# Masks of local attention scores: written into PSUM by VectorE instead of added by TensorE, and maxima taken for two heads together

## The chip, the cores and the metric

The kernel runs on one core of a Trainium2 chip. The metric is device time in microseconds (us); what is compared is the median of several runs. The engines are named as in the profile: PE is TensorE (its weight loads stand apart as PEld), DVE is VectorE, ACT is ScalarE, POOL is GpSimd, SP issues most DMAs.

## The reference

Two layers, each with three token mixers beside each other; the change touches one of them, attention over a window. There are 256 context tokens and 1024 latent tokens in 8 blocks of 128, with 8 query heads and 2 key heads of 64. A latent query sees all context keys and the latent keys at most 128 positions away, that is its own block, and parts of the block before and the block after:

```
s_win = jnp.einsum('bnigrd,bnjgd->bngrij', qb, kw).astype(jnp.float32) * scale
s_win = jnp.where(valid[None, :, None, None], s_win, NEG)
s_ctx = jnp.einsum('bnigrd,bjgd->bngrij', qb, k_c).astype(jnp.float32) * scale
p_ctx, p_win = sink_softmax(sink_g, [s_ctx, s_win])
```

`sink_softmax` is a softmax with one more logit per head. The third mixer, dense attention ("axial"), has no mask.

## The kernel before

Matrix products take fp32 operands as high and low parts, two or three products each. `attention` works through items: a pair of heads (`t`, 0 to 3) by a chunk of queries (`c`: 0 is the 256 context queries, 1 and 2 are 512 latent queries each), the window items first, then the axial ones. Layer 0 has 12 window items, layer 1, which drops the context queries, has 8; 16 window items in all have masks (`c` 1 and 2, four `t`, two layers).

`main` does an item in groups, a PSUM bank each, two banks (`psS`, 64 and 65 in the rows of the order) in turn. A masked item has 11 groups: four over context keys (512 columns, no mask), four over 384 columns for one head, and three that hold 256 columns for each of both heads. The last seven are masked. `scores` of a group issues two products (L1007, L1008) for each head, then the mask products (L1010: the identity times a bfloat16 mask of 0 and -1e30, added onto the bank), two exponentials on ACT (L1014, and L1015 rounded), and on DVE their difference `att_Pl` (L1016). The products with V (L1026) of a group follow two groups later (`LAG`). A masked 384-column group has two masks of 128 columns; a group of both heads has one mask for each head, of 128 columns, or 256 columns in one of the three groups (the last one when `c` is 1). That is 7 mask products per head, 14 an item.

`maxes` finds, for the item after, the maximum of each query's scores: rows of the same scores the other way round (L905), masked in the same manner (also L905), and a `reduce_max` on DVE (L906), in two banks (`mx`, 62 and 63) in turn, one head at a time.

`interleave` lays the steps of `main` and of the side work (`maxes` of the next item, projections of items to come) beside each other by their costs. After that a scheduler of the framework decides the final order on each engine; each engine then runs its own list in order.

Of the kernel before, what the change touches and what calls it, by code (L numbers as in the profile page):

```python
# [10 lines left out]
BF16 = mybir.dt.bfloat16  # L11
AF = mybir.ActivationFunctionType
ALU = mybir.AluOpType
# [12 lines left out]
NEG = -1e30  # L26
# [92 lines left out]
class Net:  # L119
# [26 lines left out]
    def consts(self):  # L146
# [11 lines left out]
        self.jt = c[:, C_JT:C_JT + 2]  # L158
        cb = one("cb", 512, BF16)
        self.identb = cb[:, 0:128]  # L160
        self.mask = cb[:, 128:512]
        nc.vector.tensor_copy(self.identb, self.ident)
        mk = self.tmp(384)
        self.dma(mk, I["mask"])
        nc.vector.tensor_copy(self.mask, mk)
        self.nh = one("nh", 8)
# [511 lines left out]
    def attention(self, l, ctxq, begin):  # L678
# [204 lines left out]
        def maxes(it, boundary=False):  # L883
# [3 lines left out]

            def one(h, qt, i, k0, kn, b, b0, b1):
                mt = it["mt"].rearrange("p (h q x) -> p h q x", h=2, q=4)
                ps = mx.next()  # L890
                if boundary and i not in kc:
                    x = self.tmp(kn)
                    self.dma(x, self.kd_ax[:, k0:k0 + kn])
                    kc[i] = P.get("Ph", 512, F32R)
                    nc.scalar.copy(kc[i][:, :kn], x)
                a = rows[h] if boundary else slice(0, 128)
                rhs = kc[i][a, :kn] if boundary else Kd[h][:, k0:k0 + kn]
                ops = [(ps[:, :kn], it["X"][a, h, 128 * qt:128 * qt + 128], rhs)]
                if win and i:
                    if b0 < b:  # L900
                        ops.append((ps[:, 0:128], self.identb, self.mask[:, 256:384]))
                    if b1 > b:
                        ops.append((ps[:, kn - 128:kn], self.identb, self.mask[:, 0:128]))
                for x, op in enumerate(ops):
                    nc.tensor.matmul(*op, start=x == 0, stop=x == len(ops) - 1)  # L905
                nc.vector.reduce_max(mt[:, h, qt, i:i + 1], ps[:, :kn], AX.X)  # L906

            it["ns"] = 1 if c == 0 else 2 if win else 3
            for i in range(it["ns"]):
                for qt in range(nq):  # L910
# [7 lines left out]
                    else:  # L918
                        b = 4 * (c - 1) + qt
                        b0, b1 = max(b - 1, 0), min(b + 1, 7)  # L920
                        k0, kn = 256 + 128 * b0, 128 * (b1 - b0 + 1)
                    for h in (0, 1):
                        yield kn / 1000, lambda x=(h, qt, i, k0, kn, b, b0, b1): one(*x)

# [34 lines left out]
        def groups(it):  # L959
# [7 lines left out]
            q0 = 4 * (c - 1)  # L967
            Mh, Ml = self.mask[:, 0:128], self.mask[:, 256:384]
            twos = []
            for b in range(max(q0 - 1, 0), min(q0 + 4, 7) + 1):  # L970
                lo, hi = max(b - 1, q0), min(b + 1, q0 + 3)
                if lo == hi:
                    if b < q0:
                        p = (2 + b, 0, 256, ((self.mask[:, 0:256], 0, 256),))
                    else:
                        p = (2 + b, 256, 256, ((self.mask[:, 128:384], 0, 256),))
# [15 lines left out]
        def main(it, after_scores=None):  # L992
# [5 lines left out]
            def scores(g):  # L998
# [4 lines left out]
                for (h, kt, q0, nq, ms) in g:  # L1003
# [3 lines left out]
                    nc.tensor.matmul(o, Kd[h][:, ksl], it["X"][:, h, q0:q0 + nq], start=True, stop=False)  # L1007
                    nc.tensor.matmul(o, Kl[h][kr, ksl], it["Y"][kr, h, q0:q0 + nq], start=False, stop=not ms)  # L1008
                    for i, (m, mo, mn) in enumerate(ms):
                        nc.tensor.matmul(ps[:, off + mo:off + mo + mn], self.identb, m, start=False,  # L1010
                                         stop=i == len(ms) - 1)
                    off += nq
# [512 lines left out]
```

## Time and profile before

| | |
|---|---|
| median of 3 runs | 3158.52 us (3156.61 to 3161.45) |
| the profiled execution: its time, its span | 3155.12 us, 3153.3 us |
| PE busy, PEld busy | 97%, 80% of the span |
| DVE, ACT, POOL busy | 58%, 37%, 25% |
| TensorE clock granted, mean | 0.993 of full speed |

Busy time of PE counts a product until its result is complete, so that neighbours overlap: the cost of a product is read from one start to the next. A row of the timeline gives start, duration, engine, line, operation, output<-input, shape and count; the brackets at its end say how long the engine sat idle before, and what ended that.

### The profile page before, as it was taken

The numbers are of one execution on the slowest core, as the hardware profiler recorded it, in microseconds if no ns is written. First come the engines' busy times: TensorE is split into PE (matmuls) and PEld (weight loads), VectorE is DVE, ScalarE is ACT, GpSimd is POOL, SyncE is SP. The second block draws the span as 40 slices with busy tenths as digits, with TensorE's granted clock in tenths as the row PEclk, the third lists the DMA queues.
The fourth block names the chain that finished last, engine by engine and source line by source line (L and its number), as shares of the span: only waits on it lengthen the run. The fifth ranks groups of instructions, "written<-read, shape, count | busy, mean of one in ns | idle before, by whom it ended". The sixth has DMA issues, their size and how long they took to land. (4 is left out here: it accounts for less than half of the span.)

```text
span 3153.3 us, 44619 instructions
## 1 busy us (share of the span) xinstructions
PE 3043.7 (97%) x16794; PEld 2514.3 (80%) x16794; DVE 1827.7 (58%) x3404; ACT 1180.6 (37%) x2295; POOL 773.2 (25%) x597
## 2 busy tenths in 40 slices
PE   7999989999999999999999999899999999999998
PEld 4889778887778787888887888777776777888886
DVE  5774737677875876412245674546678776753233
ACT  3311124455555555112223312134545555642231
POOL 2342541223222110111211343442222212002130
PEclk9999999999999999999999999999999999999999
DMA  6121211112111113512153121211112111143223
GB/s 245 41 65 54 71 56 33 46 46 68 44 54 44 41 45 100 157 38 67 41 200 111 53 66 60 66 56 48 44 51 66 47 38 58 44 151 97 66 66 99
DMA packets 135704, 224.10 MB, mean 71 GB/s; under 512 B 19648, under 2 KB 45248, under 8 KB 135488
## 3 DMA queue, kind: packets, MB, share of 16 engines
q1 hardware_dynamic: 126848, 207.10, 20.9%
q10 hardware_dynamic: 8640, 14.16, 1.2%
q8 instruction: 131, 2.15, 0.3%
q14 instruction: 85, 0.70, 0.1%
HBM read 181.52 MB, written 39.60 MB: 70 GB/s over the span
## 5 line engine op out<-in xcount | busy, mean ns | idle before, releaser
L323 PE MATMUL bank<-H_h,S_whi 128*128 128x512 f32 (+1 forms) x2536 | 960.1, 379 | 0.6 <-ACT H_h L415 0.6
L324 PE MATMUL bank<-H_h,S_whi 128*128 128x512 f32 (+1 forms) x2536 | 937.9, 370 | 5.7 <-DVE H_h L420 4.0
L325 PE MATMUL bank<-H_h,S_wlo 128*128 128x512 f32 (+1 forms) x2536 | 935.8, 369 | 0.0
L323 PEld LDWEIGHTS bank<-H_h,S_whi 128*128 128x128 f32 x2536 | 480.8, 190 | 80.2 <-issue 7.7
L325 PEld LDWEIGHTS bank<-H_h,S_wlo 128*128 128x128 f32 x2536 | 479.8, 189 | 77.0 <-issue 0.6
L324 PEld LDWEIGHTS bank<-H_h,S_whi 128*128 128x128 f32 x2536 | 480.9, 190 | 74.4 <-DVE H_h L420 5.1
L1016 DVE TENSOR_TENSOR att_Pl<-att_P,att_Ph 128x512 fp32r<-128x512 f32 (+1 forms) x512 | 376.9, 737 | 257.7 <-ACT att_Ph L1015 233.8
L1014 ACT ACTIVATE att_P<-bank 128x512 f32<-128x512 f32 (+1 forms) x512 | 299.1, 584 | 450.3 <-PE bank L1008 326.4
L906 DVE TENSOR_REDUCE S_s<-bank 128x1 f32<-128x256 f32 (+2 forms) x672 | 350.7, 535 | 115.2 <-PE bank L905 110.5
L303 ACT CAST S_whi<-S_raw 128x512 fp32r<-128x512 f32 x320 | 198.0, 621 | 525.7 <-PE bank L324 457.6
L1026 PE MATMUL bank<-att_Ph,att_V 128*128 128x512 f32 (+2 forms) x1152 | 332.1, 372 | 0.0
L305 POOL TENSOR_TENSOR S_wlo<-S_raw,S_whi 128x512 fp32r<-128x512 f32 x130 | 171.9, 1324 | 619.8 <-ACT S_whi L303 527.1
L1015 ACT ACTIVATE att_Ph<-bank 128x512 fp32r<-128x512 f32 (+1 forms) x512 | 297.1, 580 | 3.8 <-PE bank L905 3.1
L305 DVE TENSOR_TENSOR S_wlo<-S_raw,S_whi 128x512 fp32r<-128x512 f32 x190 | 153.7, 811 | 160.8 <-ACT S_whi L303 159.8
L905 PE MATMUL bank<-att_Kd,att_X 128*128 128x256 f32 (+2 forms) x644 | 217.0, 343 | 22.8 <-DVE S_s L906 12.0
L1026 PEld LDWEIGHTS bank<-att_Ph,att_V 128*128 128x128 f32 x1152 | 201.3, 190 | 29.6 <-issue 0.6
L1007 PE MATMUL bank<-att_X,att_Kd 128*128 128x512 f32 (+2 forms) x576 | 214.7, 373 | 0.0
L1008 PE MATMUL bank<-att_Y,att_Kl 68*128 68x512 f32 (+2 forms) x576 | 210.5, 366 | 0.3 <-DVE att_Y L955 0.3
L1026 PE MATMUL bank<-att_Pl,att_V 128*128 128x512 f32 (+2 forms) x576 | 205.3, 364 | 0.7 <-DVE att_Pl L1016 0.7
L1230 POOL TENSOR_TENSOR mrg_Y<-S_t,mrg_Y 128x512 f32<-128x512 f32 x64 | 95.8, 1496 | 423.3 <-DVE S_t L1229 423.2
L323 PE MATMUL bank<-mrg_G,S_whi 128*128 128x512 f32 (+1 forms) x480 | 176.7, 371 | 5.7 <-ACT mrg_G L1239 5.3
L1229 DVE SCALAR_TENSOR_TENSOR S_t<-S_t,bank 128x512 f32<-128x512 f32 x64 | 44.0, 687 | 235.7 <-PE bank L325 230.8
(207 smaller groups left out, 4380.8 us busy)
## 6 DMA issues: line engine op xcount, KB each, us to landing
S_raw<-in_win SPq DMA_DIRECT2D x216, 256.0 KB
S_t<-rd SPq DMA_DIRECT2D x108, 128.0 KB
gd<-S_t SPq DMA_DIRECT2D x48, 256.0 KB
thd<-att_th ACTq DMA_DIRECT2D x48, 256.0 KB
S_raw<-in_wp SPq DMA_DIRECT2D x48, 256.0 KB
S_t<-thd SPq DMA_DIRECT2D x48, 256.0 KB
init_wm<-in_wmod SPq DMA_DIRECT2D x16, 512.0 KB
retb_wg<-in_wmod SPq DMA_DIRECT2D x32, 256.0 KB
```

The lines of the kernel that those rows point to most:

```text
L305: self.weng.tensor_tensor(lw, raw, h.bitcast(F32), ALU.subtract)
L323: nc.tensor.matmul(ps[0][:, :n], a, xhi[k], start=k == 0, stop=False)
L324: nc.tensor.matmul(ps[0][:, :n], a, xlo[k], start=False, stop=False)
L325: nc.tensor.matmul(ps[0][:, :n], b, xhi[k], start=False, stop=k == kts - 1)
L905: nc.tensor.matmul(*op, start=x == 0, stop=x == len(ops) - 1)
L906: nc.vector.reduce_max(mt[:, h, qt, i:i + 1], ps[:, :kn], AX.X)
L1007: nc.tensor.matmul(o, Kd[h][:, ksl], it["X"][:, h, q0:q0 + nq], start=True, stop=False)
L1008: nc.tensor.matmul(o, Kl[h][kr, ksl], it["Y"][kr, h, q0:q0 + nq], start=False, stop=not ms)
L1014: nc.scalar.activation(p, ps[:, :off], AF.Exp, scale=0.125)
L1015: nc.scalar.activation(ph, ps[:, :off], AF.Exp, scale=0.125)
L1016: nc.vector.tensor_tensor(pl, p, f32(ph), ALU.subtract)
L1026: nc.tensor.matmul(pvb[h][:, q0:q0 + nq], Vf[:, kt, 192 * lo + 64 * h:192 * lo + 64 * h + 128], x, start=not started[h], stop=stop)
```

## The change

In `main` the mask products are gone. VectorE writes -1e30 into the bank itself, `copy_predicated` with a byte mask (`outside`) and one constant broadcast over the columns, after the group's score products and before its exponentials: 14 copies an item, 12 of 128 columns and 2 of 256. In `maxes` the masks stay products, but masked steps take both heads at once: two score products, then the masks of both, then two maxima. Three small instructions on DVE at the start make the byte mask and the constant.

```diff
+        nc.vector.tensor_copy(self.mask[:, 0:128], mk[:, 0:128])
+        nc.vector.tensor_copy(self.mask[:, 128:256], mk[:, 256:384])
+        self.outside = one("outside", 384, mybir.dt.uint8)
+        nc.vector.tensor_scalar(self.outside, mk, 0.0, None, ALU.is_lt)
+        self.neg = one("neg", 8)
+        nc.vector.memset(self.neg, NEG)
...
-            def one(h, qt, i, k0, kn, b, b0, b1):
+            def some(hs, qt, i, k0, kn, b, b0, b1):
...
-                for x, op in enumerate(ops):
-                    nc.tensor.matmul(*op, start=x == 0, stop=x == len(ops) - 1)
-                nc.vector.reduce_max(mt[:, h, qt, i:i + 1], ps[:, :kn], AX.X)
+                pss = [mx.next() for h in hs]
+                for h, ps in zip(hs, pss):
...
+                    nc.tensor.matmul(ps[:, :kn], it["X"][a, h, 128 * qt:128 * qt + 128], rhs, start=True,
+                                     stop=not masks)
+                for ps in pss:
+                    for x, (o, m) in enumerate(masks):
+                        nc.tensor.matmul(ps[:, o:o + 128], self.identb, m, start=False, stop=x == len(masks) - 1)
+                for h, ps in zip(hs, pss):
+                    nc.vector.reduce_max(mt[:, h, qt, i:i + 1], ps[:, :kn], AX.X)
...
-                    for h in (0, 1):
-                        yield kn / 1000, lambda x=(h, qt, i, k0, kn, b, b0, b1): one(*x)
+                    for hs in (((0, 1),) if win and i else ((0,), (1,))):
+                        yield len(hs) * kn / 1000, lambda x=(hs, qt, i, k0, kn, b, b0, b1): some(*x)
...
-                    nc.tensor.matmul(o, Kl[h][kr, ksl], it["Y"][kr, h, q0:q0 + nq], start=False, stop=not ms)
-                    for i, (m, mo, mn) in enumerate(ms):
-                        nc.tensor.matmul(ps[:, off + mo:off + mo + mn], self.identb, m, start=False,
-                                         stop=i == len(ms) - 1)
+                    nc.tensor.matmul(o, Kl[h][kr, ksl], it["Y"][kr, h, q0:q0 + nq], start=False, stop=True)
+                    for m, mo, mn in ms:
+                        nc.vector.copy_predicated(ps[:, off + mo:off + mo + mn], m,
+                                                  self.neg.to_broadcast([128, mn]))
```

Lines of the changed program are 6 to 11 higher: L905 becomes L911 (scores) and L915 (masks) of `maxes`, L906 becomes L917, L1007, L1008 become L1018, L1019, L1016 becomes L1027, L1026 becomes L1037; the copies are L1021.

Three places of the order show what moved. The first is PE in `maxes` of the first masked window item (bank 62 is one head, bank 63 the other). Before, a step of each head with its masks, other work between them:

```order
L905 MATMUL bank_62<-att_Kd_7_3434,att_X_4404 128x384
L905 LDWEIGHTS S_cb_126
L905 MATMUL bank_62<-S_cb_126 128x128
L905 LDWEIGHTS S_cb_126
L905 MATMUL bank_62<-S_cb_126 128x128
L1007 MATMUL bank_65<-att_X_4226,att_Kd_8_3435 128x384
L1008 MATMUL bank_65<-att_Y_6_3433,att_Kl_11_3438 128x384
```

And now:

```order
L911 MATMUL bank_62<-att_Kd_7_3439,att_X_4409 128x384
L911 MATMUL bank_63<-att_Kd_8_3440,att_X_4409 128x384
L915 LDWEIGHTS S_cb_126
L915 MATMUL bank_62<-S_cb_126 128x128
L915 LDWEIGHTS S_cb_126
L915 MATMUL bank_62<-S_cb_126 128x128
L915 LDWEIGHTS S_cb_126
L915 MATMUL bank_63<-S_cb_126 128x128
L915 LDWEIGHTS S_cb_126
L915 MATMUL bank_63<-S_cb_126 128x128
```

Runs of mask products have become fewer and longer: in the whole program before 128 runs of one, 156 of two and 2 of four; now 8 of one, 29 of two, 2 of three and 38 of four.

The second is DVE in the first item with `c` 1 of layer 0, from its first masked group on. Before:

```order
L1016 TENSOR_TENSOR att_Pl_4519<-att_P_4517,att_Ph_4518 128x384
L1089 TENSOR_TENSOR S_t_4370<-S_t_4370,S_t_4369 128x256
L906 TENSOR_REDUCE S_s_4411<-bank_62 128x1
L1016 TENSOR_TENSOR att_Pl_4539<-att_P_4537,att_Ph_4538 128x384
L906 TENSOR_REDUCE S_s_4411<-bank_63 128x1
L1016 TENSOR_TENSOR att_Pl_4562<-att_P_4560,att_Ph_4561 128x384
```

And now:

```order
L1021 COPY_PREDICATED bank_64<-S_outside_132,S_neg_134 128x128
L1100 TENSOR_TENSOR S_t_4375<-S_t_4375,S_t_4374 128x256
L1021 COPY_PREDICATED bank_64<-S_outside_132,S_neg_134 128x128
L1021 COPY_PREDICATED bank_65<-S_outside_132,S_neg_134 128x128 x2
L1027 TENSOR_TENSOR att_Pl_4524<-att_P_4522,att_Ph_4523 128x384
L917 TENSOR_REDUCE S_s_4416<-bank_62 128x1
L1027 TENSOR_TENSOR att_Pl_4543<-att_P_4541,att_Ph_4542 128x384
L917 TENSOR_REDUCE S_s_4416<-bank_63 128x1
L1021 COPY_PREDICATED bank_64<-S_outside_132,S_neg_134 128x128 x2
L917 TENSOR_REDUCE S_s_4416<-bank_62 128x1
L1027 TENSOR_TENSOR att_Pl_4567<-att_P_4565,att_Ph_4566 128x384
```

In three places of this item a group's copies and its difference stand with at most one short instruction between them, in others the next group's copies or several instructions stand there.

The third is PE at the end of the same item, between the last score products (L1008, L1019) and the first product that reads the last group's difference (`att_Pl_4714` before, `att_Pl_4719` now). Before, behind six products of an older group:

```order
L1026 MATMUL bank_66<-att_Ph_4677,att_V_3436 128x256 x2
L1026 MATMUL bank_66<-att_Pl_4678,att_V_3436 128x256
L1026 MATMUL bank_67<-att_Ph_4677,att_V_3436 128x256 x2
L1026 MATMUL bank_67<-att_Pl_4678,att_V_3436 128x256
L1026 MATMUL bank_66<-att_Ph_4713,att_V_3436 128x256 x2
L1026 MATMUL bank_67<-att_Ph_4713,att_V_3436 128x256 x2
L1007 MATMUL bank_65<-att_X_4404,att_Kd_7_3434 128x512
L1026 MATMUL bank_66<-att_Pl_4714,att_V_3436 128x256
```

And now, behind L1019 and one product of 256 columns:

```order
L1037 MATMUL bank_67<-att_Ph_4682,att_V_3441 128x256 x2
L1037 MATMUL bank_67<-att_Pl_4683,att_V_3441 128x256
L1018 MATMUL bank_65<-att_X_4409,att_Kd_7_3439 128x512
L1019 MATMUL bank_65<-att_Y_1_3433,att_Kl_10_3442 128x512
L329 MATMUL bank_61<-H_h_57_781,S_whi_4241 128x512
L330 MATMUL bank_61<-H_h_58_782,S_whi_4241 128x512
L331 MATMUL bank_61<-H_h_57_781,S_wlo_4243 128x512
L911 MATMUL bank_62<-att_Kd_7_3439,att_X_4759 128x256
L1037 MATMUL bank_66<-att_Ph_4718,att_V_3441 128x256 x2
L1037 MATMUL bank_67<-att_Ph_4718,att_V_3441 128x256 x2
L329 MATMUL bank_61<-H_h_59_787,S_whi_4241 128x512
L1037 MATMUL bank_66<-att_Pl_4719,att_V_3441 128x256
```

Products of the next item have moved in between.

## Rows read from the trace of the kernel before

**Rows 1.** Page, busy time of engines: us, share of the span, instructions.

```profile
PE 3043.7 (97%) x16794; PEld 2514.3 (80%) x16794; DVE 1827.7 (58%) x3404; ACT 1180.6 (37%) x2295; POOL 773.2 (25%) x597
```

**Rows 2.** Waits of PE, 2117 to 2405 us (layer 1, window items): total, times, longest.

```profile
PE bank L905 <- DVE S_s L906: 2.8, 4, 0.8
```

**Rows 3.** Four masked items as stretches: PE, PEld, DVE, ACT, POOL busy; clock; DMA.

```profile
485.00:518.00 33.00, 32.94 (x196) 26.86 (x195) 23.72 (x51) 16.27 (x35) 6.05 (x5) 1.00 0.10 29
518.00:546.50 28.50, 28.50 (x181) 25.07 (x180) 17.66 (x38) 16.26 (x33) 6.85 (x5) 1.00 0.14 48
2149.00:2183.00 34.00, 33.95 (x189) 27.18 (x188) 22.69 (x48) 16.48 (x34) 6.75 (x5) 1.00 0.13 40
2183.00:2218.00 35.00, 34.17 (x190) 26.98 (x189) 23.03 (x49) 17.11 (x35) 9.63 (x7) 1.00 0.18 54
```

**Rows 4.** Groups of instructions on PE by shape: the mask products of the groups.

```profile
L1010 PE MATMUL bank<-S_cb 128*128 128x128 bf16 x192 | 33.0, 226 | 0.0
L1010 PE MATMUL bank<-S_cb 128*128 128x256 bf16 x32 | 9.1, 283 | 0.0
```

**Rows 5.** Timeline of PE around two mask products (L1010) in a row.

```profile
500.31 0.33 PE L1007 MATMUL bank<-att_X,att_Kd 128*128 128x384 f32 x1
500.48 0.34 PE L1008 MATMUL bank<-att_Y,att_Kl 68*128 68x384 f32 x1
500.66 0.29 PE L1010 MATMUL bank<-S_cb 128*128 128x128 bf16 x2
...
501.19 0.34 PE L1026 MATMUL bank<-att_Pl,att_V 128*128 128x384 f32 x1
501.37 0.39 PE L323 MATMUL bank<-H_h,S_whi 128*128 128x512 f32 x1
501.60 0.40 PE L324 MATMUL bank<-H_h,S_whi 128*128 128x512 f32 x1
```

**Rows 6.** Timeline of PE around a single mask product, last group of an item.

```profile
512.05 0.28 PE L1007 MATMUL bank<-att_X,att_Kd 128*128 128x256 f32 x1
512.17 0.28 PE L1008 MATMUL bank<-att_Y,att_Kl 68*128 68x256 f32 x1
...
512.53 0.28 PE L1008 MATMUL bank<-att_Y,att_Kl 128*128 128x256 f32 x1
```

**Rows 7.** Timeline of PE around four mask products in a row.

```profile
2192.61 0.34 PE L905 MATMUL bank<-att_Kd,att_X 128*128 128x384 f32 x1
...
2193.00 0.72 PE L1026 MATMUL bank<-att_Ph,att_V 128*128 128x512 f32 x2
2193.55 0.40 PE L1026 MATMUL bank<-att_Pl,att_V 128*128 128x512 f32 x1
```

**Rows 8.** Groups on DVE by shape that read PSUM: busy, mean ns, idle before.

```profile
L906 DVE TENSOR_REDUCE S_s<-bank 128x1 f32<-128x256 f32 x320 | 128.0, 415 | 65.4 <-PE bank L905 62.5
L542 DVE SCALAR_TENSOR_TENSOR retb_Rs<-retb_Rs,S_g,bank 128x128 f32<-128x128 f32 x128 | 44.4, 347 | 37.5 <-PE bank L534 34.4
L372 DVE STREAM_TRANSPOSE S_t<-bank 128x128 f32<-128x128 f32 x41 | 12.7, 309 | 12.8 <-PE bank L364 11.9 <-ACT S_t L729 0.6
```

**Rows 9.** Timeline of a masked group in mid-item, from exponential to use.

```profile
498.01 0.49 ACT L1014 ACTIVATE att_P<-bank 128x384 f32<-128x384 f32 x1 [1.41 <-PE bank L1010]
...
498.91 0.56 DVE L1016 TENSOR_TENSOR att_Pl<-att_P,att_Ph 128x384 fp32r<-128x384 f32 x1
...
504.00 0.34 PE L1026 MATMUL bank<-att_Pl,att_V 128*128 128x384 f32 x1
```

**Rows 10.** Timeline of the last group of the item of rows 6.

```profile
513.05 0.60 ACT L1014 ACTIVATE att_P<-bank 128x512 f32<-128x512 f32 x1 [0.41 <-PE bank L1010]
...
514.16 0.69 DVE L1016 TENSOR_TENSOR att_Pl<-att_P,att_Ph 128x512 fp32r<-128x512 f32 x1 [2.01 <-ACT att_Ph L1015]
...
514.99 0.42 PE L1026 MATMUL bank<-att_Pl,att_V 128*128 128x256 f32 x2
```

**Rows 11.** Timeline of DVE, first group of both heads, item with `c` 2.

```profile
536.82 0.69 DVE L1016 TENSOR_TENSOR att_Pl<-att_P,att_Ph 128x512 fp32r<-128x512 f32 x1 [2.35 <-ACT att_Ph L1015]
```

More of the change, by code (lines that the diff above doesn't have):

```diff
@@ L158, in consts @@
         self.jt = c[:, C_JT:C_JT + 2]
-        cb = one("cb", 512, BF16)
+        cb = one("cb", 384, BF16)
         self.identb = cb[:, 0:128]
-        self.mask = cb[:, 128:512]
+        self.mask = cb[:, 128:384]
         nc.vector.tensor_copy(self.identb, self.ident)
@@ L164, in consts @@
         self.dma(mk, I["mask"])
-        nc.vector.tensor_copy(self.mask, mk)
+        nc.vector.tensor_copy(self.mask[:, 0:128], mk[:, 0:128])
[4 more added lines that the diff above has]
+        nc.vector.memset(self.neg, NEG)
+        self.neg = self.neg[:, 0:1]
         self.nh = one("nh", 8)
@@ L886, in maxes @@
             kc = {}
-            def one(h, qt, i, k0, kn, b, b0, b1):
+            def some(hs, qt, i, k0, kn, b, b0, b1):
                 mt = it["mt"].rearrange("p (h q x) -> p h q x", h=2, q=4)
-                ps = mx.next()
                 if boundary and i not in kc:
@@ L895, in one @@
                     nc.scalar.copy(kc[i][:, :kn], x)
-                a = rows[h] if boundary else slice(0, 128)
-                rhs = kc[i][a, :kn] if boundary else Kd[h][:, k0:k0 + kn]
-                ops = [(ps[:, :kn], it["X"][a, h, 128 * qt:128 * qt + 128], rhs)]
+                masks = []
                 if win and i:
                     if b0 < b:
-                        ops.append((ps[:, 0:128], self.identb, self.mask[:, 256:384]))
+                        masks.append((0, self.mask[:, 128:256]))
                     if b1 > b:
-                        ops.append((ps[:, kn - 128:kn], self.identb, self.mask[:, 0:128]))
-                for x, op in enumerate(ops):
-                    nc.tensor.matmul(*op, start=x == 0, stop=x == len(ops) - 1)
-                nc.vector.reduce_max(mt[:, h, qt, i:i + 1], ps[:, :kn], AX.X)
+                        masks.append((kn - 128, self.mask[:, 0:128]))
+                pss = [mx.next() for h in hs]
+                for h, ps in zip(hs, pss):
+                    a = rows[h] if boundary else slice(0, 128)
+                    rhs = kc[i][a, :kn] if boundary else Kd[h][:, k0:k0 + kn]
+                    nc.tensor.matmul(ps[:, :kn], it["X"][a, h, 128 * qt:128 * qt + 128], rhs, start=True,
[5 more added lines that the diff above has]
+                    nc.vector.reduce_max(mt[:, h, qt, i:i + 1], ps[:, :kn], AX.X)
             it["ns"] = 1 if c == 0 else 2 if win else 3
@@ L967, in groups @@
             q0 = 4 * (c - 1)
-            Mh, Ml = self.mask[:, 0:128], self.mask[:, 256:384]
+            Mh, Ml = self.outside[:, 0:128], self.outside[:, 256:384]
             twos = []
@@ L973, in groups @@
                     if b < q0:
-                        p = (2 + b, 0, 256, ((self.mask[:, 0:256], 0, 256),))
+                        p = (2 + b, 0, 256, ((self.outside[:, 0:256], 0, 256),))
                     else:
-                        p = (2 + b, 256, 256, ((self.mask[:, 128:384], 0, 256),))
+                        p = (2 + b, 256, 256, ((self.outside[:, 128:384], 0, 256),))
                 else:
```

## The prediction

> **What bounds the kernel now.** I read the busy times first, then the waits of PE, then the masked items as stretches, then single groups in the timeline. PE is busy for 97% of the span and DVE for 58% [rows 1]; the four items taken as stretches say the same of the place of the change: PE is busy for 34 of 35 us or all of it, DVE for 17.7 to 23.7 us of 28.5 to 35 [rows 3]. The longest sum of waits that PE has in layer 1's window items is 2.8 us, for maxima [rows 2]. So here each product that goes from PE is worth what it costs in PE's own stream, as long as DVE, which takes the work over, does not make PE wait. The prediction has these two halves.
>
> **What PE saves.** A mask product reads as 226 ns [rows 4], but products overlap, so I take start to start. Around two masks in a row, 500.31 to 501.19 is 0.88 us and holds four products of 384 columns beside them; such a product takes 0.17 to 0.18 us alone (500.31 to 500.48, 501.19 to 501.37), four 0.70, so the two masks cost 0.18 us [rows 5]. Around one mask, 512.05 to 512.53 is 0.48 us and holds three products of 256 columns at 0.12 each; the mask costs 0.12 us, though it is itself 256 wide [rows 6]. Around four, 2192.61 to 2193.55 is 0.94 us with one product of 384 columns (0.175) and two of 512 (0.23 each, 501.37 to 501.60); the four cost 0.305 us [rows 5, 7]. So a run costs about 0.06 us once, because the step into and out of it is not hidden, and 0.06 us for each mask.
>
> The order before has 128 runs of one, 156 of two and 2 of four: 15.4 + 28.1 + 0.6 = 44.1 us. The order after has 8 of one, 29 of two, 2 of three (0.245) and 38 of four: 1.0 + 5.2 + 0.5 + 11.6 = 18.3 us. PE saves 25.8 us. Of this 23 us is `main`, whose 224 products go (96 runs of one, 62 of two), and 2.8 us is the pairing in `maxes`, which removes breaks and no product. Spread over 16 items it is 1.6 us each.
>
> A rule of the Trainium skill speaks against so large a gain: in "TensorE: Matmul & The Clock Gate", section "Back-to-back issue gap", a stream of weight load and product pairs is given at about 81 ns for 128 columns, whatever stands around it. By that alone 224 products of `main` are worth an estimated 18 us, and the pairing nothing. The rows above show 120 ns for a lone mask and about 60 ns for one more, so the measured break decides, and I keep 25.8; what is left of the objection is the second rival below.
>
> **What DVE takes on.** Nothing in this trace writes PSUM under a mask. The nearest rows are DVE instructions that read PSUM: 128 columns take 309 ns in a transpose and 347 ns with two tensor operands, 256 columns 415 ns in a maximum [rows 8]. I take 0.31 us for 128 and 0.415 for 256, nearest to an operation with one stream of PSUM; the lower bound is 0.2 (half of the 256-column row), the upper 0.415 and 0.69 (a column costing twice, the latter as the 512-column instruction of rows 10). An item gets 12 x 0.31 + 2 x 0.415 = 4.55 us, 73 us in all. DVE in the four items goes from 23.7, 17.7, 22.7 and 23.0 to 28.3, 22.2, 27.2 and 27.6 us, in stretches that shrink by 1.6 us to 31.4, 26.9, 32.4 and 33.4 [rows 3]. It stays under, by 3.1 us in the tightest. The instructions at the start of the program are three short ones before any of this, and I put them at nothing: below 1 us if the start waits for DVE.
>
> **Who waits for the copies.** The exponentials of a masked group now wait for DVE; behind a copy on DVE stand maxima, and the difference of the group before or of this one. In mid-item that is covered: the difference of one such group is ready at 499.47 (498.91 + 0.56), and PE reads it at 504.00, so 4.5 us are spare, against two copies of 0.31 and one more hand-over [rows 9]. The bank of the group is let go about 0.7 us later too, which these 4.5 us cover alike, since the next use of the bank stands shortly ahead of that read. If that cover were gone, the copies would cost up to 0.7 us for each of 112 masked groups, 78 us.
>
> The last group of an item is not covered. Before, its difference ended at 514.85 and PE read it at 514.99 [rows 10]. From the last score product (512.53) to that read went 2.46 us [rows 6, 10]. Without the mask (-0.12) and with two copies of 256 columns and a hand-over of 0.1 us (+0.93) it will be 3.27 us. The new order has moved products of the next item in between: from L1019 to the read there stand, at the step lengths of rows 5 and 6, ten products of 256 columns counting L1019 itself, and six of 512, 1.2 + 1.4 = 2.6 us. PE stands for 0.7 us. That is the kind of item with `c` 1 in layer 0, four times. The same count for the other kinds (the last group of `c` 2 has copies of 128 columns, 0.62 us; so 3.06 us are needed; the orders leave 2.8, 3.4 and 2.8 us) gives 0.3, 0 and 0.3 us, four times each. Sum 5.2 us; with nothing better I take 5, between 0 (DVE earlier than I think) and 10 (each item late by another 0.3 us, the upper bound of the copies in two places).
>
> **Sum.** 25.8 - 5 = 21 us. The profiled execution of before took 3155.12 us with a span of 3153.3, and the median of the runs is 3158.52, 3.4 us above. The change should carry over to the median: 3158.5 - 21 = 3137.5, so I say 3137 us, and 3131 to 3144 for this case with the stalls at 0 to 10 and the PE saving good to 2 us.
>
> **Rivals.** *A mask product is worth only its own step.* The break of 0.06 us a run could belong to the change from fp32 to anything else and stay in another form (the score products of the next head now follow directly, and their weight loads could bind instead). Then 224 products at 0.06 us leave PE, 14 us, 32 of them wider but no dearer [rows 6], and the pairing gives nothing: 14 - 5 = 9 us, 3149 us. The flat step of "TensorE: Matmul & The Clock Gate" in the Trainium skill points the same way. Against it: the products of fp32 around masks show 0.12 and 0.175 us again right after the break [rows 5, 6].
>
> *The copies cost about twice.* With 0.6 us for 128 columns DVE in the tightest item has 32.1 us of work for 31.4 of PE, and the last group of every item is 0.6 us later: 0.6 x 16 = 9.6, plus 0.7 x 4 = 2.8 and some backlog, 14 us on top of the 5. The gain is 26 - 19 = 7 us or less, about 3153 us, no difference that can be told.
>
> *DVE becomes the bound, and it gets slower.* DVE runs in order. Where a group's copies and its difference stand next to each other, DVE does nothing during the two exponentials, 1.1 us (513.05 to 514.16) [rows 10]. If that happened at all seven masked groups of an item it would stand for 7.8 us, and the four items would take 36.1, 30.0, 35.0 and 35.4 us, 3.1, 1.5, 1.0 and 0.4 more than now: 24 us slower over four of each, 3182 us. It decides from where DVE's standing exceeds what PE leaves it, 3.1 us in the first kind and about 5 us in the others; to lose the whole gain it takes some 5 to 7 us of standing per item. For it: the order shows such neighbours in about three of seven groups. Against it: the standing is no loss while DVE is ahead of PE, and the trace shows it ahead, with 2.35 us idle before such a difference [rows 11]; the order also puts the next group's copies in the gap elsewhere.
>
> That the change would not do what it says is excluded by the order: the products are gone from PE's list.
>
> **How the numbers follow.** My forecast 60%, the cheap mask product 10%, the dear copies 15%, DVE as the bound 15%. What a measurement of this kernel can tell from no change is about 0.2%, 6.3 us. The first two are faster, as is a little of the third: faster 0.71, same 0.13, slower 0.16. The range leaves out the slower case and a few per cent below: from 3128, where no stall is left and PE saves 30 us, to 3158, which takes in the two middle cases.
>
> **What the new profile would show.** Right: L1010 is gone, PE's instructions fall by 224, the step from L1018/L1019 to the next product is 0.12 to 0.18 us, runs of masks in `maxes` cost what rows 7 show; the copies take about 0.31 and 0.415 us; masked items are 1.0 to 1.6 us shorter; PE's waits grow by about 5 us, for the differences of the last groups. Wrong: copies over 0.5 us, PE waiting in mid-item for differences, or for a bank that waits for its exponential, or for the maxima of a pair, because both banks now come free one behind the other.

## The result, and the profile after

| | before | after |
|---|---|---|
| median, in the same session | 3159.98 us (3156.61 to 3162.94, 4 runs) | 3199.86 us (3195.23 to 3204.75, 4 runs) |
| the profiled execution: time, span | 3155.12, 3153.3 us | 3204.75, 3202.9 us |

The ratio is 1.0127, 95% interval 1.0115 to 1.0140: 40 us slower, where 21 us faster was forecast and 3158 us was the upper end. That is the side of the third rival.

The page of the changed kernel, busy times, answers to [rows 1]:

```profile
span 3202.9 us, 44345 instructions
PE 3061.8 (96%) x16570; PEld 2520.4 (79%) x16570; DVE 1904.5 (59%) x3631; ACT 1178.8 (37%) x2295; POOL 775.7 (24%) x597
```

The products are gone (16570 instead of 16794), DVE has 77 us more, and yet PE is busier by 18 us, although it does less. To see where, I cut the window items of the two layers out as stretches, from their first score product to the first of the axial items. The columns are PE, PEld, DVE, ACT, POOL busy, granted clock, share and rate of DMA. First before, then after:

```profile
466.00:787.00 321.00, 316.50 (x1892) 260.85 (x1891) 230.60 (x494) 160.32 (x336) 77.41 (x59) 1.00 0.15 47
2110.00:2398.00 288.00, 283.58 (x1518) 218.00 (x1517) 197.46 (x397) 141.45 (x285) 75.42 (x55) 1.00 0.16 49
```

```profile
472.00:810.00 338.00, 315.97 (x1781) 261.72 (x1780) 263.47 (x605) 158.27 (x334) 77.51 (x59) 0.98 0.14 46
2142.00:2440.00 298.00, 278.81 (x1414) 217.75 (x1413) 238.10 (x503) 140.42 (x285) 78.03 (x55) 0.99 0.15 49
```

The window items went from 609 to 636 us, 27 us longer. The other 23 us of the 50 between these two executions (the profiled one of after is the slowest of its four) were lost outside them, where the change does nothing: 2544 us before, 2567 after. So there are two losses to explain, and one of them has nothing to do with masks.

In the window items PE now waits. Before, the longest sum of waits there was 2.8 us in layer 1 [rows 2], and in layer 0 (total, times, longest):

```profile
PE bank L905 <- DVE att_x L737: 1.8, 1, 1.8
```

After, the longest in layer 0 and then in layer 1:

```profile
PE bank L963 <- DVE S_cpt L951: 7.6, 4, 2.2
PE bank L1018 <- DVE bank L1021: 5.9, 6, 1.2
```

```profile
PE bank L1018 <- DVE bank L1021: 10.0, 9, 1.5
PE bank L370 <- DVE S_s L917: 2.8, 2, 2.0
PE bank L911 <- DVE S_s L917: 2.5, 4, 1.2
```

L963 transposes the maxima of the next item on their way into its `att_Y`; L1018 is a score product that waits for a copy into its own bank. And the copies themselves, all 224 (duration least, median, most; who waited for them):

```profile
L1021 DVE COPY_PREDICATED bank<-S_outside,S_neg x224: 259/300/1441, 502.9 to 2442.8; 128x128 f32<-128x128 uint8 x96, 128x256 f32<-128x256 uint8 x16
  ACT att_P L1025: 136.8, 65
  PEld bank L1018: 24.4, 30
  PE bank L1018: 16.0, 15
```

The median is about the forecast 0.31 us, the longest is nearly five times that. One such place, rows of DVE, POOL and ACT in the timeline (start, duration; x2 is two copies in one row):

```profile
701.14 1.74 POOL L744 TENSOR_TENSOR S_t<-S_t,att_sin 128x512 f32<-128x512 f32 x1
701.77 2.65 DVE L1021 COPY_PREDICATED bank<-S_outside,S_neg 128x128 f32<-128x128 uint8 x2
702.96 1.29 POOL L745 TENSOR_TENSOR att_x<-att_x,S_t 128x512 f32<-128x512 f32 x1
704.53 0.49 ACT L1025 ACTIVATE att_P<-bank 128x384 f32<-128x384 f32 x1 [3.55 <-DVE bank L1021]
```

Two copies take 2.65 us instead of 0.6. The first is over at 703.04, shortly after the first instruction of POOL ends (702.88), the second at 704.41, shortly after the second ends (704.25). ACT stands 3.55 us for them. 31 of the 224 copies take over 0.6 us, 34.1 us in all, and the other 193 take 62.5: together 96.6 us, against 73 forecast. Counted against the shortest of their shape, 40 copies take more than 1.4 times as long, and beside each of these 40 an instruction of GpSimd runs; 28 of the others have one beside them too and stay short.

### The profile page after: what moved, and what is told of

Read it like the earlier page. It is cut to its first block, busy times and chain, and to the rows that moved or that the text cites. A ratio compares the mean times of both kernels' runs of the same rounds, so it can differ in the third digit from the quotient of the medians.

```text
span 3202.9 us, 44345 instructions
## 1 busy us (share of the span) xinstructions
PE 3061.8 (96%) x16570; PEld 2520.4 (79%) x16570; DVE 1904.5 (59%) x3631; ACT 1178.8 (37%) x2295; POOL 775.7 (24%) x597
## 3 DMA queue, kind: packets, MB, share of 16 engines
q1 hardware_dynamic: 126848, 207.10, 20.4%
## 5 line engine op out<-in xcount | busy, mean ns | idle before, releaser
L1027 DVE TENSOR_TENSOR att_Pl<-att_P,att_Ph 128x512 fp32r<-128x512 f32 (+1 forms) x512 | 372.8, 728 | 223.2 <-ACT att_Ph L1026 208.2
L917 DVE TENSOR_REDUCE S_s<-bank 128x1 f32<-128x256 f32 (+2 forms) x672 | 348.2, 535 | 96.0 <-PE bank L911 84.8
L1037 PE MATMUL bank<-att_Ph,att_V 128*128 128x512 f32 (+2 forms) x1152 | 327.4, 366 | 0.6 <-ACT att_Ph L1026 0.5
L1026 ACT ACTIVATE att_Ph<-bank 128x512 fp32r<-128x512 f32 (+1 forms) x512 | 297.0, 580 | 0.5 <-PE bank L1037 0.3
L911 PE MATMUL bank<-att_Kd,att_X 128*128 128x256 f32 (+2 forms) x644 | 212.5, 346 | 26.6 <-DVE S_s L917 11.6
L1037 PEld LDWEIGHTS bank<-att_Ph,att_V 128*128 128x128 f32 x1152 | 206.1, 190 | 33.8 <-ACT att_Ph L1026 2.0
L1018 PE MATMUL bank<-att_X,att_Kd 128*128 128x512 f32 (+2 forms) x576 | 215.5, 375 | 16.9 <-DVE bank L1021 16.0
L1019 PE MATMUL bank<-att_Y,att_Kl 68*128 68x512 f32 (+2 forms) x576 | 212.2, 369 | 0.6 <-DVE att_Y L966 0.6
L1037 PE MATMUL bank<-att_Pl,att_V 128*128 128x512 f32 (+2 forms) x576 | 207.6, 368 | 1.3 <-DVE att_Pl L1027 1.3
```

What stands on the lines that cost most here:

```text
L911: nc.tensor.matmul(ps[:, :kn], it["X"][a, h, 128 * qt:128 * qt + 128], rhs, start=True, stop=not masks)
L1026: nc.scalar.activation(ph, ps[:, :off], AF.Exp, scale=0.125)
L1027: nc.vector.tensor_tensor(pl, p, f32(ph), ALU.subtract)
L1037: nc.tensor.matmul(pvb[h][:, q0:q0 + nq], Vf[:, kt, 192 * lo + 64 * h:192 * lo + 64 * h + 128], x, start=not started[h], stop=stop)
```

## The experiments

Runs told as "without masks" (e2, e7, e9, e13, e15) leave the masks of the groups in `main` out. Medians and intervals are of the runs of each kernel against the kernel before in the same session (its medians there: 3158 to 3160 us).

**First: is it the bank of two heads, the pairing, or VectorE as a whole?** In the timeline of after the score products of a group's second head go into the bank into which VectorE still copies for the first, and PE stands.

*e1* writes all four score products of a group first, then its copies:

```diff
-                    for m, mo, mn in ms:
-                        nc.vector.copy_predicated(ps[:, off + mo:off + mo + mn], m, ...)
+                    late += [(m, off + mo, mn) for m, mo, mn in ms]
...
+                for m, mo, mn in late:
+                    nc.vector.copy_predicated(ps[:, mo:mo + mn], m, self.neg.to_broadcast([128, mn]))
```

> The changed kernel, but in a group of both heads all four score products are issued before the copies, so that no product of the second head waits for the copy of the first. Theory A (the loss is mainly PE standing at the second head's products, which go into the bank that VectorE is copying into): the waits of L1018 on the copies, 16 us on PE and 24 us on weight loads in the changed kernel, go, and the time falls from 3200 to about 3165 us. Theory B (VectorE comes late to everything behind it on its list, copies, differences and the maxima's chain alike; the second head is only one place where it shows): a gain of 10 us or less, 3190 us or more. Theory C (the pairing of the maxima is the loss): no change, 3200 us.

Measured 3193.76 us, ratio 1.0113 (1.0092 to 1.0133). Six us came back. PE's wait for the bank is gone, but the wait for the maxima grew to 19.9 us (rows of PE's waits in e1, all stretches):

```profile
PE bank L963 <- DVE S_cpt L951: 19.9, 16, 2.0
PE bank L911 <- DVE S_s L917: 7.9, 12, 1.1
```

The shared bank is a real wait and not the main loss.

*e2* leaves the copies out, and with them the masks (and takes a smaller scale in the exponentials, so that nothing overflows):

```diff
-                    for m, mo, mn in ms:
-                        nc.vector.copy_predicated(...)
-                nc.scalar.activation(p, ps[:, :off], AF.Exp, scale=0.125)
+                nc.scalar.activation(p, ps[:, :off], AF.Exp, scale=0.0125)
```

> The changed kernel without any mask in the groups of main: no copy and no product; the exponentials take a smaller scale so that nothing overflows (the masks and that scale are left out of the computation). It shows what TensorE's saving is worth by itself. Theories A and B: the saving of about 26 us that the prediction read from the steps of PE is real and all the loss comes from the copies, 3130 to 3136 us. Theory C: 3170 us or more, since the pairing is still there. If a mask product were worth only 0.06 us: 3149 us.

Measured 3153.06 us, ratio 0.9982 (0.9970 to 0.9995): 5 us faster than before, where the saving of PE alone should have shown 26. *e3* and *e4* split the change:

```diff
-                    for hs in (((0, 1),) if win and i else ((0,), (1,))):
+                    for hs in ((0,), (1,)):
```

> The changed kernel with the maxima one head at a time again, 32 runs of one mask and 96 of two. Theories A and B: the pairing was worth 3 us of TensorE's time, 3200 us as before or a few more. Theory C: most of the loss goes, 3150 us or less.

Measured 3198.22 us, ratio 1.0128 (1.0103 to 1.0153). e4 is the kernel before with `some` in place of `one`, nothing else:

> The kernel before with only the pairing of the maxima: masks in the groups are products as before. Theories A and B: 3 us faster than before at most, 3155 to 3158 us. Theory C: 3185 us or more.

Measured 3157.35 us, ratio 0.9998 (0.9988 to 1.0008). The pairing is worth nothing that can be told, with copies or without.

**Second: why does the run without masks gain so little?** In its profiled execution the window items were 21 us shorter than before, as hoped, but everything outside them was 17 us longer; in e1, e3 and after, too, it was 16 to 22 us longer, and in e4 1 us. What e4 does not share with them is not an instruction: it is the layout. The byte mask, the constant and the shorter `cb` move all later buffers of the pools S (weights `S_whi`, `S_wlo`) and H (activations) by 160 bytes in each partition; those of other pools (`att_`, `mrg_`) stay. In the built program the first column of all of them stood at 96 modulo 128 before; after, S and H stand at 0 and the others at 96.

*e5* is the kernel before with 32 unused bytes; *e6* and *e7* are after and e2 with 96 unused bytes (24 in place of the 8), which makes the shift 256:

```diff
+        one("gap", 8)
         self.nh = one("nh", 8)
```

> The kernel before with one unused tile of 32 bytes per partition ahead of the small constants, and nothing else: all later buffers of the pools S and H lie 32 bytes further, those of the other pools stay. Theory D (the run without masks gained 4 us where 26 were saved, because the byte mask and the constant move S and H by 160 bytes, so that a product's columns and the next product's weights no longer start at the same place modulo 128 bytes; the 512-column steps then take 231 to 234 ns instead of 227, in all stages): slower by 16 to 20 us, about 3176. Rival F (the longer steps come with something else in the change, or differ from run to run anyway): same as before, 3158 within 6.

Measured 3175.43 us, ratio 1.0051 (1.0036 to 1.0066).

> The changed kernel with an unused tile of 96 bytes per partition behind its new constants, so that S and H lie 256 bytes further than before instead of 160. Theory D: 19 us faster than the changed kernel, 3181, ratio 1.007 to before. Rival F: 3200, ratio 1.0127, as the changed kernel.

Measured 3180.56 us, ratio 1.0069 (1.0054 to 1.0084).

> The run without masks in the groups (they are left out altogether, the exponential's scale is 0.0125 so that nothing overflows) with the same 96 bytes. Theory D: the whole saving of TensorE shows, 3158 - 26 = 3132 to 3137, ratio 0.992 to 0.9935. Rival F: 3153 as without the 96 bytes, ratio 0.998; then the saving was mis-sized.

Measured 3138.54 us, ratio 0.9938 (0.9924 to 0.9953). All three say layout: 16.6 us lost by it alone, 19.3 regained in after, 14.5 in the run without masks. Where it sits can be read in 24 products in a row in the merge (512 columns, columns from `mrg_G`, weights from S). Before, and then e5, each from the first of the 24 to the first product behind them:

```profile
1269.75 0.40 PE L323 MATMUL bank<-mrg_G,S_whi 128*128 128x512 f32 x1
...
1275.21 0.28 PE L323 MATMUL bank<-mrg_G,S_whi 128*128 128x256 f32 x1
```

```profile
1279.93 0.39 PE L324 MATMUL bank<-mrg_G,S_whi 128*128 128x512 f32 x1
...
1285.52 0.28 PE L324 MATMUL bank<-mrg_G,S_whi 128*128 128x256 f32 x1
```

5.46 us against 5.59: 227.5 ns a step against 232.9, at the same order and without a wait in between. Not every product is slower. Over all rows of PE (steps under 0.3 us), a step of 512 columns from `mrg_G` and S takes 227.8 ns on average before and 233.3 in e5 (some 1060 steps), but one from `H_h` and S, which moved together, 228.4 and 228.9 (some 4600). Over all 8750 steps of 512 columns the mean goes from 226.8 to 228.4 ns, 14 us in sum, and no view that lists waits shows it.

**Third: what do the copies cost, and how?** After the layout, 42.0 us lie between e6 (3180.6) and e7 (3138.5).

*e8* gives the differences of masked groups to GpSimd (padded, with e1's order):

```diff
-                nc.vector.tensor_tensor(pl, p, f32(ph), ALU.subtract)
+                (nc.gpsimd if late else nc.vector).tensor_tensor(pl, p, f32(ph), ALU.subtract)
```

> The changed kernel with the 96 bytes, the four score products of a group of both heads ahead of its copies, and the differences of masked groups on GpSimd instead of VectorE (about 1 us each for 384 columns, estimated between its rows of 785 ns for 256 and 1165 to 1553 ns for 512). Theory B (VectorE runs in order; its copies stand behind differences that wait for exponentials, and maxima behind both, so that PE waits): with the differences gone VectorE never stands for an exponential, and most of the 40 us that the copies cost beyond layout come back: 3140 to 3155, ratio 0.995 to 0.999. Rival G (the chain score, copy, exponential, bank free is itself too long by the copies and the hand-over, whoever does the difference): at most 10 us come back, 3165 to 3178, ratio 1.002 to 1.006.

Measured 3202.01 us, ratio 1.0138 (1.0119 to 1.0156): slower than without it, which neither theory gave. The copies became longer, and that showed the way:

```profile
L1025 DVE COPY_PREDICATED bank<-S_outside,S_neg 128x128 f32<-128x128 uint8 (+1 forms) x224 | 144.1, 645 | 55.8 <-PE bank L1021 52.4
```

Their mean is 645 ns, against 428 in e6 (128 columns), with GpSimd busy for 128 us more. So VectorE was relieved of the subtractions and got slower copies.

*e9* meant to keep VectorE's work and take the wait away (copies into a tile that nobody reads):

```diff
+                        nc.vector.copy_predicated(self.aside, m, self.neg.to_broadcast([128, 128]))
```

> The run without masks, padded (3138.5), plus 224 copies of 128 columns by VectorE at the same place of the program, but into a small bfloat16 tile of their own that nobody reads: VectorE has the work, and no exponential waits for it. Masks are left out of the groups. Theory B1 (VectorE's time is what costs: what it does for the copies comes late to everything else): 3160 to 3180, most of the 42 us that the real copies cost. Theory B2 (the wait costs: exponentials stand behind a copy, which stands behind a difference that stands for the exponentials before): 3138 to 3148.

Measured 3164.68 us, ratio 1.0017 (1.0008 to 1.0026), which tells neither: since nothing tied them, the scheduler put all 224 copies between 4.7 and 178.5 us, far ahead of the window items, whose length stayed that of e7 (309.7 and 278.2 us against 309.4 and 278.2). A failed experiment.

*e10* makes one copy for a whole group, over two blocks at once; *e11* also writes the difference one group later (`rest` does that of the group before); *e12* is e10 with products again in the 384-column groups:

```diff
+                if ms and len(g) == 1:
+                    o = ps[:, :384].rearrange("p (b x) -> p b x", x=128)[:, 0::2, :]
+                    nc.vector.copy_predicated(o, self.outside[:, 0:256].rearrange("p (b x) -> p b x", x=128), neg(128))
...
-                nc.vector.tensor_tensor(pl, p, f32(ph), ALU.subtract)
+                late_pl.append((pl, p, ph))
+                if len(late_pl) > 1:
+                    rest()
```

> The changed kernel, padded (3180.6), with one copy for a whole masked group instead of two: both outer blocks of a 384-column group as 2 x 128, and both heads of a group of two in one (one group of the 16 items' first kind takes two). So the score products of both heads stand ahead of it, too. 224 copies become 120. B1: the loss of 42 us over the run without masks shrinks with the copies' time, to about 20: 3155 to 3163. B2: only the shared bank's 6 us and little more come back: 3168 to 3176.

Measured 3159.33 us, ratio 1.0000 (0.9991 to 1.0009).

> The same with the difference of a masked or unmasked group written in the program one group later, behind the next group's copies, so that no copy need stand behind a difference of the group just before. B2: 10 us or more faster than the merged copies alone, 3145 to 3165. B1: within 5 us of them.

Measured 3143.40 us, ratio 0.9949 (0.9934 to 0.9964).

> Padded; masks are merged copies only in the three groups of both heads of an item (64 copies at most), and bfloat16 products as before in the four groups of 384 columns. PE keeps 64 runs of two (0.18 us each) and loses 96 lone products (0.12 each, 11.5 us), of which the run without masks suggests that three quarters show. B1: the loss falls with the copies' time to a quarter to a third, 10 us or so: 3155 to 3160, no difference. B2: the loss falls with the number of groups that wait, three of seven, some 15 us: 3162 to 3168. If hand-overs in these last groups cost nothing it is the fastest of all, 3148.

Measured 3165.13 us, ratio 1.0017 (1.0008 to 1.0027). e10 gave back 21 us, as theory B1 (time) said; e11 gave 16 more, as B2 (order) said; so both stayed open. e12 was slower than e10, with fewer copies, and came out where B2 had put it. With 64 runs of two products (at the prediction's 0.18 us each, 11.5 us) it would stand at 3150 on e7's footing, so that its 35.8 us of copies in the groups of both heads, the last of each item, cost an estimated 15 us. That makes them look like the dear ones; no run shows it by itself.

*e13* repeats e9 with copies that read the bank, so that they stay in place; *e14*, *e15* and *e16* write the differences later in the kernel before, in e7 and in e1 with the 96 bytes:

```diff
+                        nc.vector.copy_predicated(self.aside, m, ps[:, off:off + 128])
```

> The run without masks, padded (3138.5), plus 224 copies of 128 columns under a mask that read the group's bank and write a small bfloat16 tile of their own that nobody reads. So they stand where the real copies stand in VectorE's list, and wait for the score products alike, but no exponential waits for them, and no product except the one that takes the bank next. Masks are left out of the groups. Theory B1 (VectorE's time): most of the 42 us stay, 3165 to 3180. Theory B2 (the exponentials' wait for a copy that stands behind other work of VectorE): 3138 to 3150. Between: both, in that share.

Measured 3156.31 us, ratio 0.9992 (0.9982 to 1.0002): 17.8 us above e7. Its premise was wrong in one point: the framework lets the exponentials wait for these copies too (ACT for DVE L1024: 124.8 us, 72 times; in e6, for the real copies, 143.6 us, 68 times). So the chain is as in e6, and what differs is the copies. They are never long, though GpSimd works beside 69 of them: least, median, most are

```profile
L1024 DVE CAST_PREDICATED S_aside<-S_outside,bank x224: 244/286/293, 499.3 to 2401.4; 128x128 bf16<-128x128 uint8 x112
```

> The kernel before, masks as products in both places, with the differences written one group later. If the later differences help because copies stood behind them (B2): same as before, 3153 to 3162. If they help any kernel (H: VectorE's order was poor in the kernel before too, also in the groups without masks): 3145 to 3152, and the merged copies later gain nothing by their masks.

Measured 3154.92 us, ratio 0.9984 (0.9974 to 0.9994).

> The run without masks, padded, with the differences one group later; masks are left out of the groups. B2: 3138 within 5, since no copy stands behind a difference. H: 10 to 15 us faster, 3124 to 3129.

Measured 3124.21 us, ratio 0.9889 (0.9872 to 0.9905).

> The changed kernel, padded, 224 copies, the four score products of a group of both heads ahead of its copies (about 3175 by the earlier 6 us), and the differences one group later. B2: most of the loss goes, 3143 to 3158, though VectorE has as much work as before. B1: it stays within 6 us of 3175.

Measured 3170.15 us, ratio 1.0035 (1.0024 to 1.0046). The later differences give 14 us where there are no copies at all, 16 with merged ones, 10 with 224 (e1's order, worth 6 us in after, is in that), and 5 in the kernel before. So they don't gain by freeing copies, and B2 falls as an account of the 42 us; they are an improvement of their own.

*e17* and *e18* test what e8 and e13 suggest. A copy under a mask reads two tiles of SBUF, the mask and the constant; an addition of the bfloat16 mask to the bank reads one. e17 is after with additions (buffers as before), e18 is e11 with them:

```diff
-                        nc.vector.copy_predicated(ps[:, off + mo:off + mo + mn], m, self.neg.to_broadcast([128, mn]))
+                        o = ps[:, off + mo:off + mo + mn]
+                        nc.vector.tensor_tensor(o, o, m, ALU.add)
```

> The changed kernel with its 224 copies replaced by 224 additions on VectorE, bank = bank + mask, with the bfloat16 mask of the kernel before, so that each reads the bank and one tile of SBUF instead of two tiles of SBUF; the byte mask and the constant are gone, and the buffers lie as before. Theory P (copies with two operands in SBUF stand while GpSimd works, some 23 us in all over 31 copies): no addition over 0.6 us, mean 0.30 to 0.35 us, and 15 to 25 us faster than the padded changed kernel, 3156 to 3166. Rival Q (the long ones are long for what GpSimd does to the bank or to VectorE in general): the additions are as long as the copies, 3180 within 5.

Measured 3160.17 us, ratio 1.0008 (0.9995 to 1.0021): 20.4 us faster than e6. The additions, least, median, most:

```profile
L1016 DVE TENSOR_TENSOR bank<-bank,S_cb x224: 260/299/433, 507.5 to 2413.8; 128x128 f32<-128x128 f32 x96, 128x256 f32<-128x256 f32 x16
```

72 of them have an instruction of GpSimd beside them, and none is long. With the long ones most of PE's waits for the bank of two heads go, too (who waited for the additions, to compare with L1018 in after):

```profile
  PEld bank L1012: 8.2, 21
  PE bank L1012: 3.0, 3
```

> The merged copies with later differences (3143.4), with the same replacement: one addition of 2 x 128 columns for each masked group (two for one group of the first kind). Theory P: 120 operations at 0.42 instead of 0.60 us, 10 to 19 us faster, 3125 to 3133, near the run without masks and with later differences (3124). Rival Q: 3143 within 5.

Measured 3137.17 us, ratio 0.9936 (0.9916 to 0.9956): the fastest kernel here with its masks, 22 us faster than before and 63 faster than after. Against e11 it is 6 us, where theory P said 10 to 19 and Q none: outside both ranges. P was right in the operations' times (0.42 to 0.43 us for 2 x 128, none held up) and too high in what they are worth here. Its window items, in the columns of the stretches above, sum to 591 us:

```profile
467.00:782.00 315.00, 306.19 (x1781) 259.45 (x1780) 245.66 (x553) 159.76 (x335) 77.52 (x59) 0.99 0.15 48
2103.00:2379.00 276.00, 269.44 (x1410) 216.33 (x1408) 213.37 (x452) 141.37 (x286) 78.63 (x55) 1.00 0.16 51
```

## Why the prediction was wrong

**The sum, as it should have read.** The run without masks against before -20.3 us, the copies +42.0 (e6 against e7), the layout +19.3 (after against e6): +41.0 us, and 3158.8 + 41.0 = 3199.8. Forecast were -25.8, +5 and nothing. The three terms are differences along one chain of runs, so their sum fits by construction; each of them rests on its own pair of runs.

**What PE saves: right in kind, a fifth of it did not come.** 25.8 us were counted, 20.3 came, between that and the first rival's 14. Whether the pairing's 2.8 us are among them can't be told: e4 gained 0.5 us, and its interval takes in both 0 and 2.8. The 81 ns of "TensorE: Matmul & The Clock Gate" in the Trainium skill, section "Back-to-back issue gap", came to an estimated 18 us and nothing for the pairing; the page gives the 81 ns for a stream of such pairs, not for one product among others. The measured 20.3 us lies between 18 and 25.8, nearer to the 18.

**"Three short ones [...] at nothing" is the first step that failed.** The instructions at the start were indeed cheap: the first window item begins at 466.7 us in e2, which has them, and at 465.7 before. What I did not count was that a new constant moves every buffer behind it. That costs 16.6 us by itself (e5) and 19.3 in after.

**"In mid-item that is covered" is the second.** I counted 4.5 us of slack at one product with V, the latest reader of the chain, and set two copies of 0.31 us against it. But PE hardly waits for differences (1.3 us in all after, 0.7 before). It waits for the copies themselves, where the score products of a group's second head go into the bank that is being copied (L1018, 16.0 us in all), a wait that the prediction does not have, and for what stands behind the copies in VectorE's list, the maxima (L963, L917). And the 5 us of stalls at last groups, forecast for the differences, did not come in that form; that the last groups are the dear ones is likely (e12).

**The copy's duration is the third.** "0.31 us for 128 and 0.415 for 256" is about what a copy takes that GpSimd does not hold up (medians 0.30 and 0.43 in after), and what the additions of e17 and e18 take. The mean of the 128-column copies is 0.43, over the upper bound of 0.415. I chose the row that was nearest by what it reads in PSUM, and did not ask what it reads in SBUF. With its two tiles there, 31 copies stood while GpSimd worked: 96.6 us instead of 73. e17 takes one of the two operands away and leaves the places in the program, their number and what depends on them: the long ones vanish, and 20.4 of the 42 us. That it is not the instruction as such e13 shows, a copy under a mask with its data in PSUM, which GpSimd never holds up. The trace of before could have warned: the difference `att_Pl`, two tiles of SBUF as well, reads there as

```profile
L1016 DVE TENSOR_TENSOR att_Pl<-att_P,att_Ph x512: 518/692/1798, 471.6 to 2790.3; 128x512 fp32r<-128x512 f32 x148, 128x384 fp32r<-128x384 f32 x23
```

In 57 of these 512 the time is over a quarter above the median of the shape, and beside each of the 57 an instruction of GpSimd runs.

The rule stands in the Trainium skill, "SBUF — State Buffer", section "SBUF: two separate sides": an operation of VectorE with two inputs in SBUF and one of GpSimd that reads SBUF take one port in turn, the first for its whole duration. The rows at 701 us and e17 agree with it, here with up to 1.44 us for a copy of 0.30.

**The other 21.6 us.** Without the long ones, 224 operations of the forecast length still cost 21.6 us (e17 against e7). In the padded kernels what the masks cost goes with VectorE's time for them more than with the number of operations. Of each kernel: the time of copies or additions, and what it lost to the same kernel without them (e7; for later differences e15):

| | VectorE's time | loss |
|---|---|---|
| e13, 224 read copies | 63.7 us | 17.8 us |
| e17, 224 additions | 69.6 | 21.6 |
| e10, 120 merged copies | 75.6 | 20.8 |
| e6, 224 copies | 95.7 | 42.0 |
| e18, 120 merged additions, later | 53.3 | 13.0 |
| e11, 120 merged copies, later | 71.9 | 19.2 |
| e16, 224 copies, later | 108.5 | 45.9 |

Up to some 75 us each costs about 0.3 us; beyond, 0.7 (e11 to e16: 26.7 us lost for 36.6 more) to 1 (e10 to e6: 21.2 for 20.1). I read it as a slack that the first 75 us use up. That is argued from seven points, not shown, and time is not all: against e2, with the buffers not padded, after lost 46.8 us for 96.4 us of copies, and e1, in another order, 40.7 for 105.7.

How much of it is PE standing can be read. The window items of e7, e17 and e6, two stretches each:

```profile
469.00:778.00 309.00, 304.66 (x1778) 260.20 (x1778) 224.36 (x493) 159.51 (x335) 78.19 (x59) 0.99 0.15 49
2101.00:2380.00 279.00, 272.51 (x1411) 217.05 (x1409) 198.58 (x395) 141.91 (x287) 78.33 (x55) 0.99 0.16 51
```

```profile
476.20:799.70 323.50, 311.60 (x1784) 258.97 (x1783) 251.80 (x605) 157.92 (x334) 77.53 (x59) 0.99 0.15 48
2126.50:2413.50 287.00, 277.39 (x1420) 217.27 (x1418) 226.14 (x505) 140.75 (x285) 77.38 (x56) 1.00 0.16 51
```

```profile
469.20:807.30 338.10, 316.09 (x1783) 262.18 (x1782) 264.18 (x605) 158.45 (x334) 77.77 (x59) 0.98 0.14 46
2128.90:2426.00 297.10, 277.21 (x1418) 217.07 (x1415) 238.41 (x504) 140.68 (x285) 78.51 (x56) 1.00 0.15 49
```

PE stands idle (length less busy) for 10.8, 21.5 and 41.9 us in them. From e17 to e6, the long copies, that is 20.4 of the 24.7 us by which they grow; from e7 to e17 it is 10.7 of 22.5. The rest of the lower part, and which wait is behind it, stays open.

**The rivals.** "DVE becomes the bound" had the right sign and place, and nearly the right size for the window items (24 us forecast, 27 measured), which is a coincidence, since it came by another way: not by standing through exponentials, since moving the differences behind the next group's copies changed little there (e16), but by copies held up by GpSimd and by what queues behind them. "The copies cost about twice" was right for 31 of them, which took 1.1 us on average (34.1 us), and it let PE feel far too little of that.

**Still open.** Why the later differences gain 14 us without masks and only 5 in the kernel before; what makes up the other half of e17's loss; whether the last groups are the dear ones.

## What to carry to other kernels

Work taken from the bound engine is not free on the other because that one has idle time: ask what stands behind it in its list, and count both PSUM and SBUF operands when you look for the row that prices it. Where VectorE and GpSimd work side by side, choose the form with one SBUF operand (an addition onto the bank instead of a copy under a mask), and one instruction over two blocks instead of two. Whenever a change adds or drops a constant, look at stretches which it does not touch; if they got longer, pad the buffers back to where they were before judging the change.

## What the runs showed of the hardware that was not expected

- Steps of 512-column fp32 products depend on where buffers lie: 227.5 ns with `mrg_G` and `S_whi` both at 96 modulo 128 bytes, 232.9 ns with S at 0 (e5), 16.6 us over the kernel. A shift by 256 bytes restores it. Where `H_h` and S both moved to 0 the steps stayed (228.4 and 228.9 ns), so that it is not the place of S alone. Which two tiles must agree, and modulo 64 or 128, was not separated: some steps with both operands in `att_` tiles, which had not moved, became 2 to 3 ns longer too (`att_X` products followed by `att_Y` ones: 228.7 to 230.8).
- A copy under a mask of 128 columns takes 0.30 us beside no GpSimd work and up to 1.44 us beside it; with its data in PSUM and its result in SBUF never over 0.293 us (e13).
- 256 columns as 2 x 128 in one instruction take 0.42 us against 2 x 0.30.
- After PE had stood for 2.2 us for maxima (up to 624.91 us in after) the granted clock was about the lower level, 1.2 GHz, in the next 3.6 us, though PE was busy all through them; its 512-column steps took 0.42 to 0.43 us there. Then it was full again. Stretches of after, columns as above (the clock is the third number from the end):

```profile
620.00:625.40 5.40, 3.19 (x17) 2.38 (x16) 3.89 (x14) 2.24 (x7) 0.00 (x0) 1.00 0.13 50
625.40:629.00 3.60, 3.60 (x13) 2.96 (x12) 2.31 (x6) 1.59 (x6) 0.00 (x0) 0.53 0.00 0
629.00:634.00 5.00, 5.00 (x28) 4.32 (x27) 2.07 (x5) 1.57 (x3) 0.00 (x0) 1.00 0.02 3
```
